# Token rows of x and B, and the samples' outputs, by VectorE 32x32 transposes instead of TensorE ones

## The chip, the cores and the metric

The kernel runs on one core of one Trainium2 chip (trn2). The metric is device time in microseconds of one execution, as the median of the runs. A core has five engines that run side by side, each with its own queue of instructions in order: TensorE (PE; its weight loads are listed as PEld), VectorE (DVE), ScalarE (ACT), GpSimd (POOL) and SyncE (SP), which here does nothing but issue DMAs. On-chip data lie in SBUF, 128 partitions wide; TensorE writes only to PSUM, which has eight banks.

## The reference, cut to what matters

One step of a hybrid layer on 336 tokens: 16 learned meta tokens, 256 prompt tokens and 8 samples of 8 tokens. After an RMS norm, one projection gives all inputs of two branches. Branch A is a Mamba-2 scan: 64 heads of 64 values in 8 groups; a group shares B and C (128 states). x, B and C first go through a causal convolution of width 4 and a SiLU.

```python
def ssd_chunked(xs, dt, log_a, bm, cm, h0, chunk):
    ...
    acum = jnp.cumsum(log_a.astype(f32).reshape(bsz, nc, chunk, ng, hr), axis=2)
    seg = acum[:, :, :, None] - acum[:, :, None, :]
    decay = jnp.exp(jnp.where(causal, seg, -jnp.inf))
    cb = jnp.einsum('bcign,bcjgn->bcijg', cc, bc)
    wts = cb[..., None] * decay * dtc[:, :, None]
    y_diag = jnp.einsum('bcijgr,bcjgrp->bcigrp', wts, xc)
    to_end = jnp.exp(acum[:, :, -1:] - acum) * dtc
    chunk_states = jnp.einsum('bcjgr,bcjgrp,bcjgn->bcgrpn', to_end, xc, bc)
    ...
    y_off = jnp.einsum('bcign,bcgrpn->bcigrp', cc, h_in) * jnp.exp(acum)[..., None]
    y = (y_diag + y_off).reshape(bsz, length, nh, hp).astype(xs.dtype)
```

The prompt is scanned as one segment of 16 and two of 128 tokens; each sample is a segment of 8 with its own initial state `h0`, which adds `y_off`. The states are carried from chunk to chunk (`h_in`). The output is normed, gated, projected, and merged with branch B (a short gated convolution); then come an output projection, a residual and a final norm. All tensors are float32.

## The kernel before

**Layout.** Activations are kept with features on the partitions and the 336 tokens along the free dimension. A projection unit (`unit`, `proj`) makes 128 output features: two weight blocks of 128x1024, each a DMA on SP (`wblk`, L92) into one of three buffers, split into a high part by ScalarE (L94) and a low part by VectorE (L96), and then 24 matmuls a block: 16 with the high part (L111, L112) and, after them, 8 with the low one (L115).

**The scan.** Phase B (pool `pb`) runs over 8 groups. The scan of group g, the generator `ssd(g, st)`, is a list of steps, woven by `weave` between the projection units: four gate units z of group g (8 weight blocks), the output projection of group g-1 (8 blocks), and the convolved inputs of group g+1 (B, C and four x tiles, `conv_tile`, 12 blocks). `NSTEP` = 23 steps are spread over the units by their weights; `behind` puts a step's instructions after the last weight split and the last matmul traced ahead of them, on the same engines. DMAs on SP are not held back by it: the planner of the language orders them by when their data and buffers are ready and by program order, so that a load of a later step can be issued early.

**Rows.** The sums over tokens need x and B with tokens on the partitions. The tokens are cut in three chunks `CH` of 128, 128 and 80. `rows(c)` (L526 to L549) transposes the four x tiles on TensorE against the identity into one PSUM bank (L531), B into another (L533), and beside it puts the products of B and C of the chunk (L534). VectorE multiplies x by dt into `xdt[c]` (L536); ScalarE and VectorE make a high and a low part of B, `bt[c]` (L543, L544), or a plain copy for chunk 2 (L539); the products are masked into `cbm[c]` (L548). `decay(c)` makes exp of the differences, `weights(c)` multiplies it with `cbm[c]` (L563) and makes `xe` from `xdt` on GpSimd (L565), `halve(c)` splits `xe`, `state(c)` makes the chunk's state (L582), `carry(c)` decays the one before.

**Samples.** C of each sample's 8 tokens lies in a zero-padded tile `CZ` (L512). Eight matmuls with 32 columns of `CZ` against the eight initial states (L632) give outputs with tokens on the partitions, four side by side in PSUM; they are scaled by `eaY` (L635), transposed by TensorE (L646), and added to `ys` (L652). `eaY` is made once in `tables` with a selection matrix at `C_SE` (L424).

## Time and profile before

| | |
|---|---|
| median of 3 runs | 1825.38 us (1825.02 to 1825.8) |
| span of the profiled execution | 1824.0 us; the page gives no other time of it |
| PE busy | 1817.0 us, 12640 matmul records |
| DVE, ACT, POOL busy | 1136.7, 828.8, 374.8 us |
| DMA | 331.35 MB, mean 182 GB/s; the SP queue's packets take 54.6% of 16 engines' span |
| one group of the scan | about 112 us (1039 to 1151 us, say) |

The page's first part gives busy time per engine, the fourth the chain of work that ended last. In a line of the timeline the first number is the start in the span, the second the time from first start to last end, then engine, line of the program, operation, out<-in, shapes, and in brackets how long the engine was idle before and what ended that. A matmul's own duration holds its way through the array, so that matmuls in a row start much closer than they last. "SPq" rows are DMA issues: the time is the issue's, not the transfer's. In the DMA view, the last number is the median from issue to landing.

### The profile page before, as it was taken

The numbers are of one execution on the slowest core, as the hardware profiler recorded it, in microseconds if no ns is written. First come the engines' busy times: TensorE is split into PE (matmuls) and PEld (weight loads), VectorE is DVE, ScalarE is ACT, GpSimd is POOL, SyncE is SP. The second block draws the span as 40 slices with busy tenths as digits, with TensorE's granted clock in tenths as the row PEclk, the third lists the DMA queues.
The fourth block names the chain that finished last, engine by engine and source line by source line (L and its number), as shares of the span: only waits on it lengthen the run. The fifth ranks groups of instructions, "written<-read, shape, count | busy, mean of one in ns | idle before, by whom it ended". The sixth has DMA issues, their size and how long they took to land.

```text
span 1824.0 us, 31666 instructions
## 1 busy us (share of the span) xinstructions
PE 1817.0 (100%) x12640; PEld 1791.5 (98%) x12640; DVE 1136.7 (62%) x1687; ACT 828.8 (45%) x1269; POOL 374.8 (21%) x406
## 2 busy tenths in 40 slices
PE   9999999999999999999999999999999999999998
PEld 9999999999999999999999999999999999999998
DVE  7745544444543335657587787876868778776544
ACT  6433333333333334645656354564536546343543
POOL 0000000000000001143152432424334242400012
PEclk9999999999999999999999999999999999999999
DMA  7444444444444446456566574665746657576553
GB/s 256 143 152 150 151 149 149 144 152 152 156 152 161 162 162 224 151 182 230 168 201 225 174 248 150 205 215 178 244 150 217 201 167 252 159 236 213 183 176 127
DMA packets 117283, 331.35 MB, mean 182 GB/s; under 512 B 20816, under 2 KB 37904, under 8 KB 117136
## 3 DMA queue, kind: packets, MB, share of 16 engines
q1 hardware_dynamic: 116272, 327.96, 54.6%
q8 instruction: 99, 1.62, 0.3%
q10 hardware_dynamic: 864, 1.38, 0.2%
q14 instruction: 48, 0.39, 0.1%
HBM read 296.41 MB, written 32.88 MB: 181 GB/s over the span
## 4 chain that ended last, share of the span: by engine, by line
PE 98%; ACT 1%; DMA 0%; issue 0%; DVE 0%; POOLq 0%; POOL 0%; ACTq 0%; DVEq 0%
PE pj L111 30%; PE pj L112 30%; PE pj L115 30%; PE yb L642 2%; PE pj L219 1%; PE ms L632 1%; PE yb L582 1%; PE pj L857 1%; PE ms L531 1%; DMA wraw<-w 0%; PE ms L219 0%; PE yb L708 0%; PE yb L883 0%; PE ms L646 0%; PE ms L188 0%; ACT W L556 0%
## 5 line engine op out<-in xcount | busy, mean ns | idle before, releaser
L111 PE MATMUL pj<-hx,whi 128*128 128x320 f32 (+3 forms) x2880 | 864.2, 312 | 0.0
L112 PE MATMUL pj<-hx,whi 128*128 128x320 f32 (+3 forms) x2880 | 860.6, 311 | 0.0
L96 DVE TENSOR_TENSOR wlo<-wraw,whi 128x1024 fp32r<-128x1024 f32 x470 | 591.3, 1259 | 417.3 <-PE pj L115 214.8
L94 ACT ACTIVATE whi<-wraw 128x1024 fp32r<-128x1024 f32 x470 | 497.0, 1058 | 773.7 <-PE pj L112 639.6
L111 PEld LDWEIGHTS pj<-hx,whi 128*128 128x128 f32 x2880 | 540.7, 188 | 3.8 <-ACT pad L457 1.7
L112 PEld LDWEIGHTS pj<-hx,whi 128*128 128x128 f32 x2880 | 541.5, 188 | 0.1
L115 PE MATMUL pj<-hx,wlo 128*128 128x320 f32 (+3 forms) x2880 | 485.4, 310 | 0.0
L115 PEld LDWEIGHTS pj<-hx,wlo 128*128 128x128 f32 x2880 | 440.5, 188 | 0.0
L111 PE MATMUL pj<-yh,whi 128*128 128x320 f32 x512 | 153.5, 312 | 0.1
L112 PE MATMUL pj<-yl,whi 128*128 128x320 f32 x512 | 152.2, 308 | 0.0
L593 POOL TENSOR_TENSOR h<-h,decS 128x512 f32<-128x512 f32 x64 | 72.5, 1166 | 152.2 <-PE ms L632 152.2
L111 PEld LDWEIGHTS pj<-yh,whi 128*128 128x128 f32 x512 | 96.6, 189 | 1.4 <-ACT zs L498 0.4
L112 PEld LDWEIGHTS pj<-yl,whi 128*128 128x128 f32 x512 | 95.9, 187 | 0.6
L115 PE MATMUL pj<-yh,wlo 128*128 128x320 f32 x512 | 95.7, 309 | 0.0
L739 DVE TENSOR_TENSOR yan<-yan,pj 128x320 f32<-128x320 f32 x112 | 54.3, 485 | 64.6 <-PE pj L115 63.1
L242 POOL COPY SCS<-up 128x2 f32<-128x2 f32 x16 | 18.2, 1139 | 359.2 <-DVE up L236 329.0
L466 DVE SCALAR_TENSOR_TENSOR cacc<-pad,V,cacc 128x360 f32<-128x360 f32 (+1 forms) x144 | 89.0, 618 | 2.0
L115 PEld LDWEIGHTS pj<-yh,wlo 128*128 128x128 f32 x512 | 80.3, 188 | 0.0
L459 POOL COPY pad<-cs 128x24 f32<-128x24 f32 x48 | 49.5, 1032 | 128.3 <-DVE cacc L466 116.9
L111 PE MATMUL pj<-vhi,whi 128*128 128x320 f32 x256 | 75.5, 308 | 0.0
L112 PE MATMUL pj<-vlo,whi 128*128 128x320 f32 x256 | 75.5, 308 | 0.0
L460 POOL COPY cs<-pad 128x3 f32<-128x3 f32 x48 | 45.3, 944 | 81.5 <-ACT pad L457 81.1
(287 smaller groups left out, 1710.9 us busy)
## 6 DMA issues: line engine op xcount, KB each, us to landing
wraw<-w SPq DMA_DIRECT2D x346, 512.0 KB, 3.8
wraw<-wso SPq DMA_DIRECT2D x64, 512.0 KB, 3.5
wraw<-wsc SPq DMA_DIRECT2D x32, 512.0 KB, 3.7
h<-h0T SPq DMA_DIRECT2D x32, 512.0 KB, 5.5
ssms<-h SPq DMA_DIRECT2D x32, 512.0 KB, 4.3
wraw<-wo SPq DMA_DIRECT2D x32, 512.0 KB, 3.8
xq_d<-xe SPq DMA_DIRECT2D x16, 320.0 KB, 3.4
W<-ac_d SPq DMA_DIRECT2D x8, 576.0 KB, 6.5
```

The costliest lines, as they stand in the source:

```text
L94: latest["act"] = nc.scalar.activation(hi[:, :n], raw[:, :n], AF.Copy).ins
L96: latest["dve"] = nc.vector.tensor_tensor(lo[:, :n], raw[:, :n], fb(hi[:, :n]), sub).ins
L111: nc.tensor.matmul(out, w, xh(k0 + k), start=first and k == 0, stop=False)
L112: nc.tensor.matmul(out, w, xl(k0 + k), start=False, stop=False)
L115: latest["pe"] = nc.tensor.matmul(out, w, xh(k0 + k), start=False, stop=last and k == nk - 1).ins
L219: nc.tensor.matmul(pu[i][:, :T - t0], w[:, o:o + P], x[:, k, t0:], start=k == 0 and j == 0, stop=k == 15 and j == 2)
L459: nc.gpsimd.tensor_copy(smp[:, :, 0:3], cs[:, 1:9, :])
L460: nc.gpsimd.tensor_copy(cs[:, 0, :], pad[:, 272:275])
L466: nc.vector.scalar_tensor_tensor(acc[:, i0:], pad[:, i0 + k:360 + k], col(V_CW, 4 * j + k), acc[:, i0:], mult, add)
L593: nc.gpsimd.tensor_tensor(split(h0[b]), split(h0[b]), bc(hv(decS[:, b, :], g), [P, 8, HP]), mult)
L642: nc.tensor.matmul(yb[q * HP:(q + 1) * HP, t, t0:t0 + n], x[:, h * HP:(h + 1) * HP], w[:, h, :], start=i == 0, stop=i == 3)
L739: nc.vector.tensor_tensor(ya[:, m, :TV], ya[:, m, :TV], pp[:, :TV], add)
```

## The change

It takes the transposes of x, B and the samples' outputs off TensorE.

1. In `conv_tile`, after B or an x tile (128 features x 336 tokens) is made, VectorE transposes it block by block, 32x32: tokens 0 to 319 in one instruction, the last 32 in a second, into the 352 columns of the tile `acc`. This tile is written to DRAM, `xr_d`, as 4 blocks of 32 rows of 1408 bytes, by a DMA on ScalarE's queue. The DMA is held in `pend` and issued by `flush` one unit later, behind an activation of the next `conv_tile` or z unit.
2. `load(c)` reads it back by 32 tokens: for each, 32 partitions x 16 pieces of 32 floats of x into `xdt[c]`, and 32 x 4 pieces of B into `bt[c]`; 22 DMAs a group on SP, traced in the fifth step, behind `decay(1)`, which moves there from the sixth.
3. `rows(c)` is parted. `cross()` makes all three products of B and C in one PSUM bank and masks them into three tiles `cbm`; `rows_in(c)` multiplies `xdt[c]` by dt in place and splits `bt[c]`. For chunk 0 it stands ahead of `weights(0)`, for chunk 1 behind `halve(0)`, for chunk 2 behind `halve(1)`.
4. The samples' outputs are made by 32 matmuls of 128 columns, so that each 32-partition block of PSUM holds one head quarter's 32 features with the tokens in its rows; scaled over 256 columns, transposed by VectorE and added from SBUF. `CZ` and `eaY` get the layout for it; `eaY` is made by eight small matmuls with columns of the identity, and the matrix at `C_SE` goes.

```diff
+    xr_d = [dr.tile([20, 32, XR], F32, name=f"xr_d{i}") for i in range(2)]
...
-            nc.tensor.matmul(pc[:, 0:NH], CM[:80, C_SE:C_SE + P], eat[:80, 2, :], start=True, stop=True)
-            nc.vector.tensor_copy(eaY, pc[:, 0:NH])
+            for c in range(2):
+                for a in range(0, P, 32):
+                    nc.tensor.matmul(pc[a:a + 32, NH * c:NH * c + NH], ident[:80, META + 32 * c:META + 32 * c + 32],
+                                     eat[:80, 2, :], start=True, stop=True)
...
+        def flush():
+            while pend:
+                nc.scalar.dma_start(*pend.pop())
...
             nc.scalar.activation(acc[:, i0:], pad[:, i0:360], AF.Identity, bias=col(V_CB, j), scale=col(V_CW, 4 * j))
+            flush()
...
+            if rows is not None:
+                nc.vector.transpose(acc[:, :320], out[:, :320])
+                nc.vector.transpose(acc[:, 320:XR], out[:, T - 32:])
+                pend.append((rows.rearrange("a q n -> (a q) n"), acc[:, :XR]))
...
                 nc.scalar.activation(z[:, :TV], pz, AF.Copy)
+                flush()
...
-            def rows(c):
-                (t0, n), m = CH[c], NT[c]
-                pp = ps.tile([P, 512], F32, name="ms")
-                for t in range(4):
-                    nc.tensor.transpose(pp[:n, t * P:t * P + P], xs[:, t, t0:t0 + n], ident)
-                pq = ps.tile([P, 512], F32, name="ms")
-                nc.tensor.transpose(pq[:n, 0:P], BT[:, t0:t0 + n], ident)
-                nc.tensor.matmul(pq[:n, P:P + m], BT[:, t0:t0 + n], CT[:, TGT[c]:TGT[c] + m], start=True, stop=True)
...
+            def load(c):
+                xdt[c] = big("xdt", 3)
+                b = bt[c] if c == 2 else fb(bt[c][:, 1, :])
+                rows = xr_d[g % 2].rearrange("a q n -> q a n")
+                for i in range(4 if c < 2 else 3):
+                    k, a, q = 4 * c + i, 32 * i, 16 if 4 * c + i == 10 else 0
+                    for d, lo, n in ((xdt[c], 0, 16), (b, 16, 4)):
+                        nc.sync.dma_start(d[a:a + 32 - q].rearrange("p (a f) -> p a f", f=32),
+                                          rows[q:, lo:lo + n, 32 * k:32 * k + 32])
+
+            def cross():
                 pq = ps.tile([P, 512], F32, name="ms")
+                o = 0
+                for c, (t0, n) in enumerate(CH):
+...
+                    nc.tensor.matmul(q, BT[:, t0:t0 + n], CT[:, TGT[c]:TGT[c] + m], start=True, stop=True)
+                    cbm[c] = pb.tile([P, m], F32, name=f"cbm{c}", bufs=1)
+...
+            def rows_in(c):
+                n = CH[c][1]
+                nc.vector.tensor_tensor(split(xdt[c][:n]), split(xdt[c][:n]), bc(hv(dtt[:n, c, :], g), [n, 8, HP]), mult)
+                if c < 2:
+                    b = fb(bt[c][:, 1, :])
+                    nc.scalar.activation(bt[c][:, 0, :], b, AF.Copy)
+                    nc.vector.tensor_tensor(bt[c][:, 1, :], b, fb(bt[c][:, 0, :]), sub)
...
             yield
-            rows(0)
+            cross()
             yield
             decay(0)
             yield
             nc.scalar.activation(E, W[1], AF.Exp)
-            rows(1)
...
             yield
+            decay(1)
+            for c in range(3):
+                load(c)
+            yield
+            rows_in(0)
             weights(0)
             yield
             halve(0)
-            decay(1)
-            yield
-            rows(2)
+            rows_in(1)
             yield
             carry(0)
             state(0, pieces(0))
             weights(1)
             yield
             halve(1)
+            rows_in(2)
             decay(2)
...
-            for s_ in range(2):
-                for q in range(4):
-                    nc.tensor.matmul(po[32 * q:32 * q + 32], CZ[:, 64 * q + 32 * s_:64 * q + 32 * s_ + 32],
-                                     h0[2 * q + s_], start=s_ == 0, stop=s_ == 1)
+            for b in range(NB):
+                z = 160 * (b // 4) + 32 * (b % 4)
+                for a in range(4):
+                    nc.tensor.matmul(po[32 * a:32 * a + 32, P * (b // 4):P * (b // 4) + P], CZ[:, z:z + 32],
+                                     h0[b].rearrange("p (t a f) -> p a t f", a=4, f=32)[:, a],
+                                     start=b % 4 == 0, stop=b % 4 == 3)
...
+            nc.vector.transpose(yo[:, 256:], yo[:, :256])
...
-            for t in range(4):
-                nc.tensor.transpose(pt_[:, t * P:t * P + P], yo[:, t * P:t * P + P], ident)
...
+            sy = ys[:, :, 272:].rearrange("p t (s q) -> p t s q", q=32)
+            nc.vector.tensor_tensor(sy, sy, yo[:, 256:].rearrange("p (s t q) -> p t s q", s=2, t=4), add)
```

More of the change, by code (lines that the diff above doesn't have):

```diff
@@ L164, in tile_hybrid_step @@
     eat = keep.tile([P, 3, NH], F32, name="eat")
-    eaY = keep.tile([P, NH], F32, name="eaY")
+    eaY = keep.tile([P, 2, NH // 2], F32, name="eaY")
     cdec = keep.tile([P, 2, NH], F32, name="cdec")
@@ L423, in tables @@
             pc = ps.tile([P, 512], F32, name="ms")
-            nc.tensor.matmul(pc[:, 0:NH], CM[:80, C_SE:C_SE + P], eat[:80, 2, :], start=True, stop=True)
-            nc.vector.tensor_copy(eaY, pc[:, 0:NH])
+            for c in range(2):
+                for a in range(0, P, 32):
+                    nc.tensor.matmul(pc[a:a + 32, NH * c:NH * c + NH], ident[:80, META + 32 * c:META + 32 * c + 32],
+                                     eat[:80, 2, :], start=True, stop=True)
+            for i in range(2):
+                nc.vector.tensor_copy(eaY[64 * i:64 * i + 64], pc[64 * i:64 * i + 64, :2 * NH].rearrange(
+                    "p (c h i) -> p i c h", c=2, i=2)[:, i])
             yield
@@ L447, in tile_hybrid_step, with conv_tile @@
         npad = [0]
-        CZ = pb.tile([P, 256], F32, name="CZ", bufs=1)
+        CZ = pb.tile([P, 320], F32, name="CZ", bufs=1)
         nc.gpsimd.memset(CZ, 0.0)
-        czs = CZ.rearrange("p (q w) -> p q w", w=64)
-        def conv_tile(src, j, t0, out, cs):
+        czs = CZ.rearrange("p (s i w) -> p s i w", s=2, w=40)
+        pend = []
+        def flush():
+            while pend:
+                nc.scalar.dma_start(*pend.pop())
+        def conv_tile(src, j, t0, out, cs, rows=None):
             pp = proj(src, t0)
@@ L517, in ssd @@
             ys = pb.tile([P, 4, T], F32, name="ys", bufs=1)
-            W, xdt, xe, bt, cbm, hst = ([None] * 3 for _ in range(6))
+            W, xdt, xe, cbm, hst = ([None] * 3 for _ in range(5))
             W[0], W[1] = (pb.tile([P, 8, PX], F32, name="W")[:, :, :n] for n in (P - META, PX))
@@ new lines, in ssd @@
+            bt = [pb.tile([P, 2, P], F32R, name="bh0", bufs=1), free[:, 1024:1280].rearrange("p (i n) -> p i n", n=P),
+                  pb.tile([P, P], F32, name="bt", bufs=1)]
+            def load(c):
[7 more added lines that the diff above has]
+                                          rows[q:, lo:lo + n, 32 * k:32 * k + 32])
@@ new lines, in cross @@
+            def cross():
+                pq = ps.tile([P, 512], F32, name="ms")
+                o = 0
+                for c, (t0, n) in enumerate(CH):
+                    m = NT[c]
+                    q = pq[:n, o:o + m]
+                    o += m
+                    nc.tensor.matmul(q, BT[:, t0:t0 + n], CT[:, TGT[c]:TGT[c] + m], start=True, stop=True)
+                    cbm[c] = pb.tile([P, m], F32, name=f"cbm{c}", bufs=1)
+                    u0 = META if c == 0 else 0
+                    for a, b, to in ((0, m, 0),) if c < 2 else ((META, 80, 0), (0, META, 64)):
+                        nc.vector.tensor_tensor(cbm[c][:n, to:to + b - a], q[:, a:b],
+                                                U[:, u0 + a:u0 + b] if c < 2 else UQ[:, a:b], mult)
```

44 lines of the change are left out of this document (12 added, 32 removed).

## The prediction

> **What bounds the kernel now.** I read the page first (busy shares, granted clock, chain), then the stretch 1039 to 1151 us, one of eight like groups.
>
> ```profile
> PE 1817.0 (100%) x12640; PEld 1791.5 (98%) x12640; DVE 1136.7 (62%) x1687; ACT 828.8 (45%) x1269; POOL 374.8 (21%) x406
> PEclk9999999999999999999999999999999999999999
> PE 98%; ACT 1%; DMA 0%; issue 0%; DVE 0%; POOLq 0%; POOL 0%; ACTq 0%; DVEq 0%
> 1039.00:1151.00 112.00, 112.00 (x797) 108.99 (x796) 85.83 (x134) 58.46 (x100) 41.37 (x42) 1.00 0.61 199
> ```
>
> TensorE (PE) is busy for 1817.0 of 1824.0 us at full clock, and the chain of waits lies on it for 98%. In a group's 112 us it has no gap, while DVE works 85.8 and the DMA engines 61%. A matmul taken away shortens the run by its pitch, unless a wait fills the place. So I need the pitch of what goes, and the margins of the engines that get work.
>
> **What goes from PE.** Next the groups of the lines in question, and PE's timeline (start, duration) around `rows(1)` and the samples' output of one group.
>
> ```profile
> L531 PE MATMUL ms<-CR,xs x96: 270/272/273, 751.9 to 1550.4; 128*128 128x128 f32 x64, 128*80 128x128 f32 x32
> L533 PE MATMUL ms<-CR,BT x24: 272/273/273, 752.4 to 1550.5; 128*128 128x128 f32 x16, 128*80 128x128 f32 x8
> L646 PE MATMUL ms<-CR,xe x32: 272/273/328, 803.1 to 1579.5; 128*128 128x128 f32 x32
> ...
> 1095.04 0.60 PE L531 MATMUL ms<-CR,xs 128*128 128x128 f32 x4
> 1095.47 0.27 PE L533 MATMUL ms<-CR,BT 128*128 128x128 f32 x1
> 1095.58 0.41 PE L534 MATMUL ms<-CT,BT 128*128 128x144 f32 x2
> ...
> 1133.25 1.92 PE L632 MATMUL ms<-h,CZ 128*32 128x512 f32 x16
> 1135.11 0.66 PE L642 MATMUL yb<-W,xdt 128*64 128x112 f32 x8
> 1138.56 0.66 PE L646 MATMUL ms<-CR,xe 128*128 128x128 f32 x4
> 1138.97 0.40 PE L111 MATMUL pj<-hx,whi 128*128 128x336 f32 x1
> ```
>
> The 272 ns are latency; the pitch counts. From 1095.04 to 1095.58 five transposes take 0.54 us: 108 ns each. L646's four take 0.41. The counts, 96 + 24 + 32, are 152 transposes, 19 a group: 19 x 0.108 = 2.05 us, times 8 = **16.4 us** removed. The products of B and C (L534) stay, gathered in `cross()`.
>
> **The samples' state product (L632)** becomes 32 matmuls of 128 columns instead of 8 of 512: the same columns in 64 records (each float32 matmul is two) instead of 16. Now the block takes 1135.11 - 1133.25 = 1.86 us for 4 rounds of 4 records side by side, 0.46 a round. Lower bound: 16 rounds at a quarter of that, 1.86, no change. Upper bound: L642's pace, whose 64 records take 1138.56 - 1135.11 = 3.45 us, 54 ns each: 64 x 54 ns = 3.45, 1.6 more a group, 12.7 us in all. I take 0: L642's 54 ns are mostly streaming, and the records of a round already run side by side.
>
> The Trainium skill ("TensorE: Matmul & The Clock Gate", "Wait — 56ns, not 53.3ns?") gives a floor of about 25 ns start to start, or 62 ns per MATMUL when its sequencer decodes in software. By 25 ns the estimate stays at no change; by 62 ns, 64 x 62 = 4.0 us, 2.1 more a group, and the whole gain is gone. The trace's 54 ns over 64 records speak against the 62.
>
> In `tables`, once, one 64-column matmul becomes eight, four side by side: I add 0.1 us.
>
> **What DVE gains.** For B and the four x tiles, a transpose of 128x320 and one of 128x32 follow each convolution. No such instruction is in the trace. DVE is tightest here:
>
> ```profile
> 1051.77 0.49 DVE L696 TENSOR_SCALAR ms_x<-ms 128x320 f32<-128x320 f32 x1 [1.11 <-ACT ms_r L695]
> ...
> 1056.96 0.44 DVE L470 SCALAR_TENSOR_TENSOR xs<-cth,cacc 128x272 f32<-128x272 f32 x1
> ...
> 1063.55 0.44 DVE L470 SCALAR_TENSOR_TENSOR xs<-cth,cacc 128x272 f32<-128x272 f32 x1
> 1063.90 0.22 DVE L471 SCALAR_TENSOR_TENSOR xs<-cth,cacc 128x64 f32<-128x64 f32 x1
> ...
> 1065.36 1.22 DVE L96 TENSOR_TENSOR wlo<-wraw,whi 128x1024 fp32r<-128x1024 f32 x1
> ...
> 1067.64 1.39 PE L115 MATMUL pj<-hx,wlo 128*128 128x336 f32 x8
> ```
>
> From 1051.77 on DVE's rows follow without a gap; the weight block's low half is ready at 1066.58 and PE takes it up at 1067.64: 1.06 us of margin. Two x tiles end in this run, so two pairs of transposes come ahead of L96. By the 128x320 row (0.49) and the 128x64 row (0.22, about 0.14 to the next start) a pair is some 0.5, two are 1.0: just covered. At half that, nothing; at twice, 2.0, PE stalls 0.9 a group for seven groups, 6.6 us. I take 0, as these are plain passes of the same width. The rest of DVE's change is small: `rows_in` multiplies in SBUF what L536 multiplied from PSUM, and the output's second transpose takes the place of nothing on PE's path, since `ys` is wanted much later.
>
> **ScalarE** loses a copy (L539, chunk 2's B) and gains five DMA issues a group. Each waits for the transposes of the tile before, queued one unit later, so ACT's splits behind it are hardly held; by SP's rows an issue is 0.3 to 0.5 us, 2.5 at most in 112 of which ACT works 58. That is cover enough.
>
> **The loads** are the real risk. Per group: 22 DMAs on SP, 336 tokens x 20 pieces = 6720 pieces of 128 bytes. They need the last x tile, whose write is issued behind ACT's z copy (L498). Around that point:
>
> ```profile
> 1082.21 0.43 ACT L498 ACTIVATE zs<-pj 128x320 f32<-128x320 f32 x1
> ...
> 1083.31 1.63 SPq L604 DMA_DIRECT2D h<-h0T  x2
> 1085.04 0.38 SPq L92 DMA_DIRECT2D wraw<-w  x1
> 1086.49 0.33 SPq L92 DMA_DIRECT2D wraw<-wso  x1
> 1086.87 1.01 SPq L478 DMA_DIRECT2D cs<-convst  x1
> 1090.11 9.81 SPq L92 DMA_DIRECT2D wraw<-wso  x3
> ...
> 1093.32 1.06 ACT L94 ACTIVATE whi<-wraw 128x1024 fp32r<-128x1024 f32 x1 [4.84 <-DMA wraw<-w]
> ...
> 1094.41 1.23 DVE L96 TENSOR_TENSOR wlo<-wraw,whi 128x1024 fp32r<-128x1024 f32 x1 [2.95 <-ACT whi L94]
> 1095.56 2.18 DVE L563 TENSOR_TENSOR W<-W,cbm 128x896 f32<-128x896 f32 x1
> 1098.33 1.23 DVE L96 TENSOR_TENSOR wlo<-wraw,whi 128x1024 fp32r<-128x1024 f32 x1 [0.60 <-ACT whi L94]
> ...
> 1104.05 0.75 PE L115 MATMUL pj<-yh,wlo 128*128 128x320 f32 x4
> 1108.31 0.75 PE L115 MATMUL pj<-yh,wlo 128*128 128x320 f32 x4
> ```
>
> ```profile
> DMA packets 771, 0.35 MB, mean 202 GB/s; under 512 B 768, under 2 KB 768, under 8 KB 771
> q1 hardware_dynamic: 771, 0.35, 71.4%
> xh<-xq_d SPq DMA_DIRECT2D x16, 256.0 KB, 4.1
> SPq L92 <- DMA wraw<-w: 20.6, 12, 2.8
> ```
>
> The DMA view is of 1488.25 to 1490, when almost only W's 448-byte rows move: 768 packets in 1.75 us are 439 per us. At this pace 6720 pieces take 15.3 us; scaled by bytes (128/448) 4.4. I expect 8, nearer the short end, as the engines were busy 71% of that time with packets 3.5 times as long. SP's own issuing takes 22 x 0.4 to 0.53 (two xh issues took 1.06 together), 9 to 12 us, so the weight issue of 1090.11 goes out at 1098 or so.
>
> When do they land? The write is issued at 1082.7 and is there by 1087. ACT's wait at 1093.32 shows the queue still delivering what was issued at 1085. So chunk 0's eight DMAs (2560 pieces) come in from about 1094, in 2 to 6 us: 1096 to 1100. `rows_in(0)` and `weights(0)` would stand on DVE where L563 stands, at 1095.56, and wait 0.5 to 4.5 us. Behind them is the low half now done at 1099.56, wanted by PE at 1104.05: 4.5 us of cover, less 0.7 for the multiply moved there. The weight block sent at 1098 instead of 1090 lands near 1102 to 1105; ACT's split (1.06) ends by 1106; PE starts it 1.2 before 1108.31, at 1107.1. Both margins hold by a little. I take 0.2 us of stall for each of seven groups, 1.4 (bounds 0 and 4 a group, in the rivals). If the loads are still later, the late thing is first DVE's low half, then the state product of chunk 0.
>
> Moving `decay(1)` ahead of `halve(0)` and the loads changes only ACT's order within one gap; `czs` needs one POOL copy less.
>
> **Sum.** The page gives no time of the profiled execution beside its span, 1824.0; the runs' median, 1825.38, is 1.4 above. Span: 1824.0 - 16.4 + 0.1 + 1.4 = 1809.1; with the 1.4 around it, **1810.5 us**.
>
> **Rivals.**
>
> *Loads a little later.* With the long price of a piece, DVE waits until 1100, and the weights and the low half each come about 1.2 us after PE wants them. 8 x 1.2 = 9.6 in place of 1.4: 1818.7. For it: ACT already waits up to 4.84 us for weights in this stretch. Against it: the planner moves DMAs forward wherever data and buffers allow (B's half is written five units earlier).
>
> *SP's queue is held (the other side).* The row "SPq L92 <- DMA wraw<-w" shows SP waiting up to 2.8 us for the landing of an earlier weight DMA although the buffer is freed by DVE: the number of transfers under way is limited, and no moment of this trace has more than eight. 22 small loads are then three rounds of a landing each, 4.1 by the xh row and more under load, say 5.2: 15.6 us from 1087, and the weights of 1090.11 go out at 1103, land at 1108.5 with the pieces still moving, are split at 1109.6 or later, and PE, due at 1107.1, stalls 2.5 to 5. From a stall of 2.05 us a group on the gain is gone; at 3.75 it is 8 x 3.75 - 16.3 = 13.7 slower, 1839. For it: 22 DMAs in one place, and DMA busy already. Against: about 5 us of cover on both engines.
>
> The Trainium skill ("DMA: Bandwidth & Descriptors", "Rules for kernel authors") speaks for this rival: coalesce small transfers, since below 64 KB one pays mostly overhead; each load here is 64 or 16 KB. The trace agrees that a small load lands no sooner than a weight block.
>
> *Small matmuls at 54 ns a record*: 1810.5 + 12.7 = 1823.2.
>
> *No effect.* The place of the transposes fills with waits, so the change doesn't do what it says: 1825. Against it: no gap on PE today, and all waits of its operands have margin.
>
> **How the numbers follow.** Forecast 0.50, own range 1808 to 1814 (the half and the double of DVE's price, 0 to 0.5 of stall); loads late 0.22; SP held 0.16; no effect 0.07; small matmuls 0.05. What a measurement here tells from no change is about 0.2%, 3.7 us. Faster than 1821.7: 0.50 + 0.22 = 0.72. Same: 0.07 + 0.05 = 0.12. Slower: 0.16. The range, 1807.5 to 1824, takes the forecast, the late loads and the small matmuls, and leaves out the held queue and half of the no-effect case; its low end is the full 16.4 with the first L646's longer step (0.06 a group, by its row of up to 328 ns) and no stall, 1808.6, less 1 us for what another set of runs may differ by.
>
> **What would show it.** Right: no 128x128 transposes on PE in the scan, PE busy some 16 us less with the idle time unchanged at 7 us, the state product still 1.9 us a group, a transpose pair near 0.5 us. Wrong: PE waiting in front of the units L111 or L115 for ACT or DVE once a group, behind a DVE or ACT wait for xdt's DMA; SP holding weight issues behind the loads for over 12 us; a state product of 3 us.

## The result, and the profile after

The changed kernel takes 1891.07 us (median of four runs, 1889.84 to 1895.21) against 1825.22 before in the same session. The ratio is 1.0363, with a 95% interval of 1.0350 to 1.0375: slower by 66 us, where 1810.5 was forecast. The changed program's lines are numbered anew: weight DMA L94, its ScalarE part `whi` L96, its VectorE part `wlo` L98, matmuls L113, L114 (high) and L117 (low), products of `cross()` L565, their masks L569, row loads L555, rows times dt L574, z units L516 (tanh), L517 and L519, and L773, the `yan` additions of VectorE that take a finished PSUM tile of the output projection and free it. In the kernels of the experiments these numbers shift by a few lines.

The page of the changed kernel, whose span is 1888.5 us: busy times, and the granted clock in 40 slices:

```profile
PE 1833.5 (97%) x12886; PEld 1809.0 (96%) x12886; DVE 1183.9 (63%) x1776; ACT 828.8 (44%) x1261; POOL 376.6 (20%) x398
PEclk9999999999999999999999989999999999999999
```

TensorE's idle time went from 7 us (1824.0 - 1817.0) to 55 (1888.5 - 1833.5). And its busy time *rose* by 16.5 us although 152 transposes had left it. The waits of TensorE say where the idle time is (who waits for whom, total us, times, longest):

```profile
PE ms L565 <- DVE cbm L569: 23.4, 14, 2.4
PE pj L113 <- ACT whi L96: 15.1, 9, 1.8
PE pj L113 <- DVE yan L773: 7.8, 5, 1.6
PE pj L113 <- ACT zs L517: 1.9, 1, 1.9
```

So there are two places, both new. **The products**: 23.4 us, twice a group in seven groups, ahead of the second and third product of `cross()`. **The weight pieces** (the first matmuls of a weight block): 15.1 + 7.8 + 1.9 = 24.8 us, once or twice a group, nearly all just behind the last z unit. Together 48.2 us.

The first place, on the timeline of the group at 1104 us:

```profile
1104.84 0.37 PE L565 MATMUL ms<-CT,BT 128*128 128x112 f32 x2
...
1106.45 1.22 DVE L98 TENSOR_TENSOR wlo<-wraw,whi 128x1024 fp32r<-128x1024 f32 x1 [0.56 <-ACT whi L96]
1107.55 2.63 POOL L596 TENSOR_TENSOR E<-E,CT 128x1152 f32<-128x1152 f32 x1 [7.58 <-ACT E L629]
1107.60 0.27 DVE L569 TENSOR_TENSOR cbm<-ms,CR 128x112 f32<-128x112 f32 x1
1107.92 0.51 PE L565 MATMUL ms<-CT,BT 128*128 128x144 f32 x2 [2.11 <-DVE cbm L569]
1108.15 2.38 DVE L519 SCALAR_TENSOR_TENSOR zs<-cth,zs 128x320 f32<-128x320 f32 x1 [0.29 <-ACT zs L517]
1110.45 0.30 DVE L569 TENSOR_TENSOR cbm<-ms,CR 128x144 f32<-128x144 f32 x1
1110.80 0.55 PE L565 MATMUL ms<-CT,BT 128*80 128x80 f32 x2 [1.74 <-DVE cbm L569]
1113.37 2.33 PE L117 MATMUL pj<-hx,wlo 128*128 128x320 f32 x8
```

The first product is done at 1105.2. Its mask stands in VectorE's queue behind a weight split and runs at 1107.60. Only then does the second product start, in the same PSUM tile but other columns; then the same once more, this time behind a z product of VectorE that takes 2.38 us while GpSimd works (0.48 is its usual time). The last row shows what follows: eight low-half matmuls take 2.33 us where eight take 1.39 in the prediction's row of before, with some more columns. The windows around it (length, PE busy, granted clock, DMA share, GB/s):

```profile
1108.00:1110.00 2.00, 1.07 (x6) 0.71 1.08 285
1110.00:1112.00 2.00, 1.20 (x5) 0.50 0.56 77
1112.00:1114.00 2.00, 2.00 (x9) 0.50 0.39 62
1114.00:1116.00 2.00, 2.00 (x10) 0.59 0.58 91
```

The granted clock falls to 0.50 for some 7 us and is back at 1.00 from 1116 on. The list of cores gives its mean over the span: 0.983, where it was 0.999 before. So 1888.5 x 0.017 = 32 us are lost to the clock against 2. The account of the 64.5 us between the two spans: - 16.2 for the transposes (2.03 a group, shown further on) + 48.2 idle + 30 clock = + 62; 2.5 stay unassigned.

The second place, as rows of SyncE's, ScalarE's and TensorE's timelines of that group:

```profile
1106.29 9.47 SPq L555 DMA_DIRECT2D xdt<-xr_d  x11
1115.86 1.52 SPq L94 DMA_DIRECT2D wraw<-wso  x3
...
1126.31 0.44 ACT L516 ACTIVATE cth<-pj 128x320 f32<-128x320 f32 x1 [6.25 <-PE pj L117]
1126.96 1.06 ACT L96 ACTIVATE whi<-wraw 128x1024 fp32r<-128x1024 f32 x1
...
1128.07 0.41 PE L113 MATMUL pj<-yh,whi 128*128 128x320 f32 x1 [1.80 <-ACT whi L96]
1134.99 0.39 PE L113 MATMUL pj<-yh,whi 128*128 128x320 f32 x1 [1.53 <-DVE yan L773]
```

Eleven loads of x rows take SyncE 9.5 us, and the first weights of the output projection (`wso`) are issued behind them, 12.2 us ahead of the first matmul that uses them, its gap included; in before it is 16.4 us, from the issue at 1086.49 to the first such matmul at 1102.87. Their split stands in ScalarE's order *behind* the tanh of the last z tile, which must wait for TensorE: ScalarE is idle for 6.25 us, and TensorE then for 1.80.

### The profile page after: what moved, and what is told of

It is laid out like the page before. It is cut to its first block, busy times and chain, and to the rows that moved or that the text cites. A ratio compares the mean times of both kernels' runs of the same rounds, so it can differ in the third digit from the quotient of the medians.

```text
span 1888.5 us, 32627 instructions
## 1 busy us (share of the span) xinstructions
PE 1833.5 (97%) x12886; PEld 1809.0 (96%) x12886; DVE 1183.9 (63%) x1776; ACT 828.8 (44%) x1261; POOL 376.6 (20%) x398
## 4 chain that ended last, share of the span: by engine, by line
PE 87%; DVE 5%; ACT 3%; DMA 3%; issue 2%; SPq 0%; POOLq 0%; DVEq 0%; POOL 0%; ACTq 0%
PE pj L113 27%; PE pj L117 27%; PE pj L114 27%; DMA wraw<-w 2%; PE yb L679 1%; ACT whi L96 1%; DVE h L745 1%; DVE zs L519 1%; DVE wlo L98 1%; PE ms L665 1%; PE pj L221 1%; DVE cacc L480 1%; PE yb L611 1%; DVE xdt L574 1%; PE pj L891 0%
## 5 line engine op out<-in xcount | busy, mean ns | idle before, releaser
L113 PE MATMUL pj<-hx,whi 128*128 128x320 f32 (+3 forms) x2880 | 870.9, 314 | 4.3 <-ACT whi L96 4.3
L114 PE MATMUL pj<-hx,whi 128*128 128x320 f32 (+3 forms) x2880 | 866.3, 313 | 0.0
L98 DVE TENSOR_TENSOR wlo<-wraw,whi 128x1024 fp32r<-128x1024 f32 x470 | 598.1, 1274 | 378.7 <-PE pj L117 201.7
L96 ACT ACTIVATE whi<-wraw 128x1024 fp32r<-128x1024 f32 x470 | 496.0, 1058 | 751.3 <-PE pj L114 609.7
L113 PEld LDWEIGHTS pj<-hx,whi 128*128 128x128 f32 x2880 | 545.4, 189 | 9.5 <-ACT whi L96 5.0
L114 PEld LDWEIGHTS pj<-hx,whi 128*128 128x128 f32 x2880 | 546.2, 190 | 0.1
L117 PE MATMUL pj<-hx,wlo 128*128 128x320 f32 (+3 forms) x2880 | 491.0, 313 | 0.0
L117 PEld LDWEIGHTS pj<-hx,wlo 128*128 128x128 f32 x2880 | 445.3, 190 | 0.7
L113 PE MATMUL pj<-yh,whi 128*128 128x320 f32 x512 | 158.5, 320 | 20.5 <-ACT whi L96 10.8
L114 PE MATMUL pj<-yl,whi 128*128 128x320 f32 x512 | 157.0, 317 | 0.0
L113 PEld LDWEIGHTS pj<-yh,whi 128*128 128x128 f32 x512 | 100.2, 196 | 24.8 <-ACT whi L96 12.4
L114 PEld LDWEIGHTS pj<-yl,whi 128*128 128x128 f32 x512 | 100.1, 196 | 0.7
L117 PE MATMUL pj<-yh,wlo 128*128 128x320 f32 x512 | 99.9, 318 | 0.0
L472 POOL COPY pad<-cs 128x24 f32<-128x24 f32 x48 | 61.4, 1280 | 141.4 <-DVE cacc L480 116.3
L773 DVE TENSOR_TENSOR yan<-yan,pj 128x320 f32<-128x320 f32 x112 | 54.2, 484 | 54.5 <-PE pj L117 53.0
L117 PEld LDWEIGHTS pj<-yh,wlo 128*128 128x128 f32 x512 | 83.9, 196 | 0.2
L113 PE MATMUL pj<-vhi,whi 128*128 128x320 f32 x256 | 75.5, 308 | 0.0
L114 PE MATMUL pj<-vlo,whi 128*128 128x320 f32 x256 | 75.5, 308 | 0.0
L519 DVE SCALAR_TENSOR_TENSOR zs<-cth,zs 128x320 f32<-128x320 f32 x32 | 27.9, 871 | 65.2 <-ACT zs L517 64.8
```

The source lines that it names most:

```text
L96: latest["act"] = nc.scalar.activation(hi[:, :n], raw[:, :n], AF.Copy).ins
L98: latest["dve"] = nc.vector.tensor_tensor(lo[:, :n], raw[:, :n], fb(hi[:, :n]), sub).ins
L113: nc.tensor.matmul(out, w, xh(k0 + k), start=first and k == 0, stop=False)
L114: nc.tensor.matmul(out, w, xl(k0 + k), start=False, stop=False)
L117: latest["pe"] = nc.tensor.matmul(out, w, xh(k0 + k), start=False, stop=last and k == nk - 1).ins
L472: nc.gpsimd.tensor_copy(smp[:, :, 0:3], cs[:, 1:9, :])
```

## The experiments

**1. The products first.** My theory: the two places are independent, and the clock follows the gaps. First, `cross()` with its three products ahead of the masks:

```diff
                 nc.tensor.matmul(q, BT[:, t0:t0 + n], CT[:, TGT[c]:TGT[c] + m], start=True, stop=True)
+                    qs.append((c, n, m, q))
+                for c, n, m, q in qs:
                     cbm[c] = pb.tile([P, m], F32, name=f"cbm{c}", bufs=1)
```

> The changed kernel with one edit: the three products of a group are issued one behind the other, and the masks follow; nothing else is touched. Theory: the changed kernel loses 23.4 us of TensorE idle because the second and third product wait for VectorE's mask of the one before, which shares its PSUM tile, and 24.8 us because the output projection's weight pieces are split late; TensorE's busy time rose by 16.5 us although 16.4 us of transposes left, so 32.9 us are a lower clock behind those 48.2 us of gaps, 0.68 us for each. The products' gaps go and their clock with them: 1891 - 23.4 x 1.68 = 1852 us. Rival A (the clock is held down by something other than the gaps): only the idle time comes back, 1868 us. Rival B (the weights are late in any case, so TensorE stands still a little later for as long): 1885 to 1891 us, and the idle at the weight pieces grows by some 20 us.

Measured: 1855.41 us, ratio 1.0173 (1.0156 to 1.0190). Rows of the groups:

```profile
L113 PE MATMUL pj<-hx,whi 128*128 128x320 f32 (+3 forms) x2880 | 864.7, 312 | 6.5 <-ACT whi L96 6.5
L113 PE MATMUL pj<-yh,whi 128*128 128x320 f32 x512 | 157.6, 319 | 24.3 <-DVE yan L775 13.3 <-ACT whi L96 10.8 <-ACT yan L773 0.2
L565 PE MATMUL ms<-CT,BT 128*128 128x112 f32 (+2 forms) x48 | 6.2, 265 | 0.0
```

The products wait for nothing now (23.4 to 0.0), the clock rises to 0.994, and 35.7 us come back. Rival B allowed 6 and rival A, the gaps alone, 23.4; the theory said 39. The weight pieces' 24.8 us became 30.8, so it seems that a part of the wait moved there.

**2. The gathered products alone**, in the kernel before:

```diff
             yield
+            cross()
             rows(0)
```

(`rows(c)` without its product and masks, all else as before.)

> The kernel before with one part of the change alone: the three products of a group gathered into one step and one PSUM tile with the masks between them, as the change has it; transposes, rows and samples' outputs as before. Theory: two gaps a group of 1.0 to 2.4 us appear ahead of the second and third product and the clock falls behind them: 1825 + 23.4 x 1.68 = 1865 us. Rival (the mask comes late only because VectorE's order is upset by the rows that are read back): VectorE does each mask as soon as its product is done, gaps of 0.6 to 0.9 us, 16 of them, 10 to 14 us with no more than as much clock: 1837 to 1848 us. Rival (the clock has another cause): 1825 + 23 = 1848 us with the clock at 1.00.

Measured: 1839.80, ratio 1.0077 (1.0062 to 1.0092). Its group row, and windows around two of its gaps (PE busy, clock, DMA share, GB/s):

```profile
L552 PE MATMUL ms<-CT,BT 128*128 128x112 f32 (+2 forms) x48 | 9.5, 279 | 11.6 <-DVE cbm L556 11.5
...
1096.00:1098.00 2.00, 2.00 (x12) 0.61 0.94 369
1098.00:1100.00 2.00, 2.00 (x9) 0.54 0.05 20
...
1550.00:1552.00 2.00, 0.42 (x3) 1.00 0.97 365
1552.00:1554.00 2.00, 2.00 (x17) 1.00 0.96 363
```

This one part costs 14.4 us in a kernel with nothing else changed: the size of the first rival, not my 40, though by other gaps than it said. There is one a group, seven of 1.25 to 2.10 us, and just one of them (2.10, at 1095) is followed by the low clock. The gap of 1.92 at 1551 isn't. So my price of 0.68 us of clock for each us of gap was wrong as a rule: in these traces the clock's loss comes in pieces, and not behind every gap (last section).

**3. The samples' outputs alone**, in the kernel before (part 4 of the change, with `eaY` and `CZ`).

> The kernel before with one part of the change alone: the samples' outputs by 32x32 transposes on VectorE, with the state product cut into 128-column pieces; x and B rows as before. Theory: 32 transposes of 108 ns leave TensorE, 3.5 us, the state product keeps its 1.9 us a group, one VectorE transpose of about 0.4 us is covered: 1825.2 - 3.5 = 1821.8 us. Rival (the small matmuls cost 54 ns each instead of 30): 1834 us. Rival (VectorE's transpose stands between the product and what follows): TensorE waits once a group, 1826 to 1832 us.

Measured: 1823.99, ratio 0.9990 (0.9981 to 1.0000): 1.4 us gained of 3.5 forecast. The interval just reaches no change, but all ten runs (1823.0 to 1824.7) lie below the thirteen of before (1824.99 to 1827.07). TensorE's idle time is 0.3 us more. A group without a wait is 0.36 us shorter (111.44 us between state products, 111.80 before), 2.9 us in eight; against that the first state product starts 0.4 us later, and two of the groups are 0.3 and 0.7 us longer than the others. The state product is 15.6 us in all against 15.4 before, so the small matmuls cost nothing, as forecast.

**4. The loads on ScalarE's queue**, in the changed kernel:

```diff
-                        nc.sync.dma_start(d[a:a + 32 - q].rearrange("p (a f) -> p a f", f=32),
+                        nc.scalar.dma_start(d[a:a + 32 - q].rearrange("p (a f) -> p a f", f=32),
```

> The changed kernel with one edit: the 22 loads of rows a group are issued by ScalarE's queue instead of SyncE's. Theory (the weight pieces are late because SyncE's queue is held for 9.5 us by eleven loads ahead of them, and the pieces are then split behind the last z tile): SyncE's weight issues come some 9 us earlier, most of the 24.8 us of idle at the weight pieces goes with 0.68 us of clock for each: about 1850 us, the products' gaps of 23.4 us unchanged. Rival (the transfers themselves are late by contention of small packets, whoever issues them): 1885 to 1895 us. Rival (ScalarE is now held by its 22 issues of 0.45 us, and splits weights late): 1895 us or more, TensorE waiting for ScalarE.

Measured: 1951.39, ratio 1.0691 (1.0674 to 1.0708), clock 0.969. The second rival. ScalarE's timeline:

```profile
1156.22 0.31 ACT L577 ACTIVATE bh<-bh 128x128 fp32r<-128x128 f32 x1 [7.25 <-DMA xdt<-xr_d]
```

For 7.25 us it issues loads, and the split of TensorE's next weights, at 1156.43, stands behind them: a gap of 8.8 to 9.7 us in each group.

**5. Queue or order?** From here on the kernels have the products first (1855.41 us is what to compare with), but for two in the last experiment. Three loads' steps instead of one; then, the other way, the first `wso` block fetched and split ahead of the last z tile's last matmuls:

```diff
             decay(1)
-            for c in range(3):
-                load(c)
+            load(0)
             yield
             rows_in(0)
             weights(0)
+            load(1)
...
+            load(2)
             carry(0)
```

```diff
             hi, lo = wblk(src[:, half * 1024:half * 1024 + 1024])
+            if half and hook:
+                hook()
...
+            def ahead():
+                S[g - 1]["w"] = wblk(wso[g - 1, 0])
```

> The kernel with the three products first (1855 us, 30.8 us of TensorE idle, all of it at the weight pieces), and one edit more: the rows of the three token groups are loaded in three steps of the scan instead of one, so that SyncE's queue never holds more than four x loads in a row. Theory (eleven x loads in a row, 9 us, hold the weight issues behind them): the first weights of the output projection are issued 5 to 6 us earlier, the idle at the weight pieces falls from 30.8 to 5 to 15 us, about 1832 us. Rival (the split is late because ScalarE's order has it behind the last z tile's activations, whenever the weights land): 30 us of idle stay, 1850 to 1857 us. Rival (the scan's later steps now wait for rows that land late): TensorE waits at the state products, over 1857 us.

> The kernel with the three products first, and one edit more: the first weights of the output projection are fetched and split ahead of the last z tile's last matmuls in the program's order, so that their ScalarE copy can stand ahead of that tile's activations. Theory of the order (ScalarE's order alone makes the gap of 1.80 us, once a group): these eight gaps, 14.4 us, go, and some of what follows: 1835 to 1842 us. Theory of the queue (the weights themselves are issued late, behind eleven x loads): they land no earlier, ScalarE now waits for them with the z tile's activations behind it, the gaps stay at 1 us or more: 1848 to 1858 us.

> Products first, loads in three steps, and the first weights of the output projection ahead of the last z tile's activations. With the loads spread alone, these weights had landed some 3 us before ScalarE took them up and the gaps of 1.80 us stayed (1859.6 us); with the order alone they were late (1842.8 us, idle 22 us). If queue and order each hold back one part: idle under 10 us, 1820 to 1828 us. If the order alone counts: as with the order alone, 1840 to 1845 us.

Measured: spread 1859.62 (1.0190, 1.0174 to 1.0205); ahead 1842.78 (1.0098, 1.0083 to 1.0113); both 1839.20 (1.0074, 1.0061 to 1.0088), with 21 us of idle at the weight pieces and the clock at 0.999. The spread kernel, SyncE's, ScalarE's and TensorE's rows:

```profile
1102.11 1.29 SPq L94 DMA_DIRECT2D wraw<-wso  x2
...
1109.17 0.44 ACT L516 ACTIVATE cth<-pj 128x320 f32<-128x320 f32 x1 [2.46 <-PE pj L117]
1109.82 1.06 ACT L96 ACTIVATE whi<-wraw 128x1024 fp32r<-128x1024 f32 x1
...
1110.93 0.41 PE L113 MATMUL pj<-yh,whi 128*128 128x320 f32 x1 [1.80 <-ACT whi L96]
```

Here the first weights were issued at 1102.1; the DMA view of that moment (1102.0 to 1102.5) has 3.9 us to their landing, so they lay there at 1106.0. Yet their split came at 1109.82, behind a z tile that ScalarE had waited 2.46 us for. The gap is the same 1.80. So in this kernel the *order* of ScalarE's queue makes that gap. The other edit wins 12.6 us, just above the range of its theory, but it turns more than that order: the first weights now go out at 1095.24, ahead of the eleven loads (from 1095.61 on), so that queue and order aren't parted by it. And neither edit nor both bring the idle time under 20 us; for both I had expected 1820 to 1828.

**6. Other ways to carry the rows.** The scatter into rows of tokens done by the write (ScalarE's queue, four transfers a tile), so that SyncE reads whole rows with eight loads; and GpSimd's queue for the 22 loads; each also with the order turned.

```diff
+                for a in range(4):
+                    pend.append((rows[:, 32 * a:32 * a + 32].rearrange("(k q) f -> q k f", q=32),
+                                 acc[32 * a:32 * a + 32, :XR].rearrange("q (k f) -> q k f", f=32)))
...
-                        nc.sync.dma_start(d[a:a + 32 - q].rearrange("p (a f) -> p a f", f=32),
+                        nc.gpsimd.dma_start(d[a:a + 32 - q].rearrange("p (a f) -> p a f", f=32),
```

> The kernel with the three products first, and one edit more: the scatter of 128 B pieces is moved from the read to the write. ScalarE's queue writes each tile in four transfers, straight to rows of tokens, spread over the convolution's tiles, and SyncE reads whole rows of 2048 and 512 B in eight loads a group instead of 22, four of them of x instead of eleven. Theory (SyncE's queue is held by the eleven x loads): held 2 us instead of 9, idle at the weight pieces from 30.8 to under 8 us with the clock back at 0.999: 1812 to 1822 us, below the kernel before. Rival (ScalarE's 20 issues of 0.32 us instead of five stand in the splits' way): 4.8 us of issues more a group on an engine that is 45% busy, TensorE waits 1 to 2 us a tile: 1840 to 1870 us. Rival (order on ScalarE, as above): 1850 us.

> The scatter moved to the write and the first weights of the output projection fetched and split ahead of the last z tile's last matmuls, both. If queue and order each hold back one part, this one has neither: no idle at the weight pieces, 1810 to 1814 us, TensorE's busy time about 1805 us. If one of the two alone made the gaps, it equals the run with that one edit within 3 us.

> Products first, and the 22 row loads of a group issued by GpSimd's queue instead of SyncE's. Theory (eleven x loads in a row hold SyncE's weight issues): the first weights of the output projection are issued right behind those of the last z tile, 9 us earlier, idle at the weight pieces from 30.8 to under 8 us: 1812 to 1825 us. Rival (the order on ScalarE makes the gaps whenever the weights land): the gaps of 1.80 us stay, eight of them, 14 us with some clock: 1838 to 1850 us. Rival (GpSimd's issues are dear, or its own products stand behind loads that wait for the rows to be written): xe and the products with E come late, TensorE waits at the state products or at the outputs: over 1850 us.

> Products first, row loads on GpSimd's queue, and the first weights of the output projection ahead of the last z tile's activations. By the theory of queue and order: no idle over 3 us in all, TensorE's busy time 1803 to 1807 us: 1810 to 1814 us, below the kernel before. By the theory of the queue alone: equal to the run with GpSimd's queue alone within 3 us. By GpSimd held: over 1850 us.

Measured: scatter 1886.31 (1.0331) and 1877.67 with the order; GpSimd 1871.31 (1.0246) and 1874.40 with the order. My theory missed all four; the two on GpSimd's queue lie in the rival that had over 1850 us, the scatter in none. SyncE's waits in the scatter kernel, and GpSimd's issues in the other (busy us, mean ns, idle before):

```profile
SPq L556 <- DMA xr_d<-cacc: 91.0, 18, 9.3
```

```profile
L555 POOL DMA_DIRECT2D xdt<-xr_d x88 | 56.0, 642 | 85.1 <-DMA h<-h0T 50.4 <-DMA xdt<-xr_d 18.2 <-DMA xr_d<-cacc 14.1
```

With fewer loads SyncE stands at them for 91 us in all, up to 9.3 at a time, until the rows are written; the weights stand behind. GpSimd stands still for 85 us ahead of the x loads, with its own work in order behind them. TensorE's waits in that kernel are put down to ScalarE's z copies (20.6 us) and VectorE's `yan` (16.1), not to GpSimd; how they come from its queue was not followed.

**7. Late rows?** Rows written a group earlier (nothing to wait for, and so x and B of another group in the states); the first use of the rows three steps later; the last x tile left to TensorE.

```diff
-                rows = xr_d[g % 2].rearrange("a q n -> q a n")
+                rows = xr_d[(g + 1) % 2].rearrange("a q n -> q a n")
```

> The kernel with the products first, and the 22 loads of a group read the rows that the group before left in DRAM (group 0 writes both buffers), so that x and B enter the scan's states with the rows of another group: the amount of work, the queues and the sizes stay, only the wait for rows just written goes. Theory (the rows land too late: written 1090.5, in DRAM 1095, loaded 1096 to 1105, multiplied from 1108): the loads are issued some 10 us earlier, ScalarE and VectorE no longer stand at the rows, idle from 30.8 to under 5 us: 1811 to 1818 us. Rival (22 loads of 128 B pieces hold SyncE's queue wherever they stand): the idle moves and stays above 15 us, 1835 to 1855 us.

> The kernel with the products first, and three empty steps between the loads and the first use of the rows; the scan has 26 steps instead of 23, and the first product with the rows stands behind the second block of the output projection instead of behind the last z tile. Theory (rows too late): 14 us more for them to land, so the splits of the first weights have no row step ahead of them: idle from 30.8 to 5 to 12 us, 1815 to 1832 us. Rival (SyncE's queue and ScalarE's order behind the last z tile): the gaps of 1.80 us stay, 1840 to 1855 us.

> The kernel with the products first, and the last of the four x tiles turned by TensorE as before, three transposes of 108 ns a group (2.6 us in all); the other three tiles and B by VectorE and the loads, each x load three quarters of its size. Theory (rows too late, and it is the tile written last that sets it): the rows are complete in DRAM 10 us earlier, the loads go out before the weights of the last z tile, idle from 30.8 to under 10 us: 1814 to 1828 us. Rival (number of loads): 1845 to 1858 us.

Measured: 1848.74 (1.0121), 1908.90 (1.0454) and 1850.20 (1.0135). The theory that the rows land too late falls: without that wait there are still 28.7 us of idle, where there were 30.8. They move, though: in the first of these kernels 18.5 us lie at the weights of the convolution and z units, where loads now stand between SyncE's weight issues. Three later steps made it worse, beyond both theory and rival: 63.8 us of idle, 23.3 of them for the low halves of VectorE. With one x tile left to TensorE 25.2 us stay, the time in the range of the rival.

```profile
L113 PE MATMUL pj<-hx,whi 128*128 128x320 f32 (+3 forms) x2880 | 868.0, 313 | 18.5 <-ACT whi L96 18.5
```

**8. x left out; the loads without the use; the use without the loads.** First the kernel before with part 4 and with B's rows as changed, but x's rows by TensorE (B loaded in the scan's first step). On it, x written and loaded as well, into a buffer that nobody reads. And from the other side, the kernel with the products first, with x neither transposed, written nor loaded:

```diff
-                nc.tensor.transpose(pq[:n, 0:P], BT[:, t0:t0 + n], ident)
+            for c in range(3):
+                load(c)
```

```diff
+            for c in range(3):
+                load_x(c)
             weights(0)
```

```diff
-                    for d, lo, n in ((xdt[c], 0, 16), (b, 16, 4)):
+                    for d, lo, n in ((b, 16, 4),):
...
-                nc.vector.tensor_tensor(split(xdt[c][:n]), split(xdt[c][:n]), bc(hv(dtt[:n, c, :], g), [n, 8, HP]), mult)
+                nc.vector.tensor_tensor(xdt[c][:n].rearrange("p (t u e) -> p t u e", u=2, e=HP),
+                                        xs[:n, :, t0:t0 + P].rearrange("p t (u e) -> p t u e", u=2),
```

> The kernel before with the samples' outputs and the rows of B as the change has them, B's rows loaded at the scan's first step; x stays with TensorE's transposes, and each product stays in its own chunk's step. Theory (it is the x rows, written just before the scan, and the gathered products that cost; B's rows are written a whole convolution earlier and nothing waits for them): 56 of the 152 transposes leave TensorE, 6 us less, no idle: 1825.3 - 6 = 1819 us, with the samples' part having given 1.4 of its 3.5 us perhaps 1821 us. Rival (any row load on SyncE's queue delays weights): idle at the weight pieces of 1 to 2 us a group, 1826 to 1840 us.

> The kernel with B's rows and the samples' outputs as the change has them (1821.7 us, no idle), and the x rows written and loaded too, at the step where the scan first uses x, into a buffer that nobody reads (the third token group's loads are cut to 320 columns); the scan goes on with TensorE's transposes of x. Theory Q (the eleven x loads hold SyncE's queue ahead of the weights, and weights issued late find no slack): 20 to 30 us of idle at the weight pieces, 1842 to 1855 us. Theory U (what costs is the use of the rows: ScalarE and VectorE stand at steps that need them, with weight splits behind): 1821 to 1826 us, no idle.

> The kernel with the products first, without the x rows' VectorE transposes, writes and loads: the scan multiplies the x tiles as they lie in SBUF, untransposed, in the rows' place (so the scan's results are not the reference's); B's rows, the steps and everything else as changed. Theory Q: no idle, TensorE busy about 1803 us, 1808 to 1814 us. Theory U: ScalarE and VectorE still run the new step order, idle of 15 to 30 us stays, 1828 to 1850 us.

Measured: **1821.67 us without x** (eleven runs, ratio 0.9979, 0.9970 to 0.9988): faster than both kernels, with 0.5 us of idle at the weight pieces. With x loaded and unused 1844.09 (1.0100, 1.0083 to 1.0117). With x used and not loaded 1836.09 (1.0059, 1.0036 to 1.0082). TensorE's waits in the second, and in the third at the output projection:

```profile
L113 PE MATMUL pj<-hx,whi 128*128 128x320 f32 (+3 forms) x2880 | 865.5, 312 | 4.4 <-ACT whi L96 4.4
L113 PE MATMUL pj<-yh,whi 128*128 128x320 f32 x512 | 156.1, 316 | 11.0 <-ACT whi L96 10.8 <-DVE yan L776 0.2
```

```profile
L113 PE MATMUL pj<-yh,whi 128*128 128x320 f32 x512 | 156.5, 317 | 14.1 <-DVE yan L779 13.0 <-ACT zs L517 1.2
```

Neither theory has it alone; each has one half. Writing and loading x, used by nobody, makes 15.4 us of idle, all but 0.2 for ScalarE's splits. The use, with no x loaded, makes 14.1, nearly all for VectorE's `yan`. Together 29.5, against 30.8 in the kernel that has both, and there the two waits are of these sizes by name as well: 17.3 for the splits and 13.3 for `yan`. This fits that no single edit above removed it. The two halves come from kernels with different steps, so that the sum comes out may be in part chance.

How loads that nobody reads make ScalarE late is in the queues of one group, first in the kernel that loads x, then in the one without x:

```profile
1093.36 7.93 SPq L560 DMA_DIRECT2D ys<-xr_d  x11
1106.81 0.44 ACT L515 ACTIVATE cth<-pj 128x320 f32<-128x320 f32 x1 [1.98 <-PE pj L117]
1107.46 2.95 ACT L96 ACTIVATE whi<-wraw 128x1024 fp32r<-128x1024 f32 x3
```

```profile
1100.05 1.06 ACT L96 ACTIVATE whi<-wraw 128x1024 fp32r<-128x1024 f32 x1 [1.26 <-PE pj L114]
1101.27 0.41 ACT L515 ACTIVATE cth<-pj 128x320 f32<-128x320 f32 x1
```

With the loads, the first weights of the output projection go out at 1101.38, behind all eleven, and three splits stand behind the last z tile's tanh. Without them these weights go out at 1085.37, and the splits (1095.10, 1097.74, 1100.05) stand ahead of that tanh. So the loads change both the issue and the order, and the spread kernel above shows that the order is enough for the gap. Why the planner turns it is in no trace.

What the use costs VectorE is in its groups (busy us, mean ns), the first line before, the others in the kernel that uses x and loads none; under them two rows of that kernel's timeline:

```profile
L536 DVE TENSOR_TENSOR xdt<-ms,dtt 128x512 f32<-128x512 f32 x16 | 10.9, 680 | 0.0
L577 DVE TENSOR_TENSOR xdt<-xs,dtt 128x512 f32<-128x512 f32 x16 | 18.7, 1170 | 0.0
L584 DVE TENSOR_TENSOR bh<-bh 128x128 fp32r<-128x128 f32 x8 | 8.2, 1029 | 0.0
...
1097.89 1.82 POOL L606 TENSOR_TENSOR xw<-xe,xw 128x512 fp32r<-128x512 f32 x1 [2.12 <-ACT xw L605]
1098.47 1.80 DVE L577 TENSOR_TENSOR xdt<-xs,dtt 128x512 f32<-128x512 f32 x1
```

The multiply by dt costs 7.8 us more, and the split of chunk 0's B, 2.2 us in before (274 ns each), 6.0. Reading x from SBUF instead of PSUM is not dearer by itself: alone, the multiply takes 0.69 us, as before. In seven of the eight groups chunk 1's starts while GpSimd works, and then it takes 1.80; so does the split of B (1.13 us beside GpSimd, 0.29 in the one group where GpSimd is nearly done). The `yan` additions, which read one operand from PSUM, take 0.48 us alone and beside GpSimd alike (88 and 24 of them). That fits that the operand's move out of PSUM lets GpSimd hold VectorE up, but in before no multiply by dt ran beside GpSimd, so for the multiply itself no run shows it. In the rows of this group VectorE works without a gap from 1097.33 until it comes to `yan` at 1105.80, and TensorE goes on at 1106.33. That these 13.8 us *are* the 14.1 of idle is not shown. The run with the use alone moved the order of the steps as well, and more work on VectorE does not make TensorE wait by itself: in the kernel without x the split of chunk 1's B takes 2.69 us a group instead of 0.28, 19 us more in all, with 0.5 us of idle. Where the work stands ahead of `yan` counts as well. The z product of VectorE, which took 2.38 us in the changed kernel's row at 1108.15, has little part in it: its mean is 481 ns in before, 871 in the changed kernel, and 519 here.

## Why the prediction was wrong

**The transposes: right.** A group without gaps takes 109.78 us in the kernel that uses x without loading it (none of the 19 transposes is left), and 111.81 before: 2.03 less, for 19 transposes at 108 ns forecast as 2.05. The starts of two successive state products, in that kernel and in the kernel before:

```profile
796.47 0.32 PE L671 MATMUL ms<-h,CZ 128*32 128x128 f32 x4
...
906.25 0.41 PE L671 MATMUL ms<-h,CZ 128*32 128x128 f32 x6
```

```profile
797.83 0.64 PE L632 MATMUL ms<-h,CZ 128*32 128x512 f32 x4
...
909.64 0.64 PE L632 MATMUL ms<-h,CZ 128*32 128x512 f32 x4
```

**The state product, the VectorE transposes, ScalarE's five issues: right.** The state product takes 15.6 us in all against 15.4; a pair of transposes takes 0.50 + 0.17 us, a third over the 0.5 forecast, and an issue 0.33; none of TensorE's waits names them.

**The step that failed first: the products "stay, gathered", at no cost.** I counted the matmuls and not the order in which they stand with their masks. Gathering three products into one PSUM tile, each followed by its mask, makes the next matmul wait for VectorE. I named no wait, no rival and no price there; it is 23.4 us of idle, and without it the changed kernel is 36 us faster, the clock included; alone, in the kernel before, it costs 14.4. The Trainium skill had a warning that I hadn't drawn on ("PSUM — Partial Sum Buffer", "PSUM bank collisions raise a hardware error"): TensorE's write and another engine's read of one bank must be kept apart by bank (strictly, by bank and block of 32 partitions), not by address. The trace fits it: the products write other columns than the masks read, and wait all the same, 14 times. That the program waits is shown; what the chip would do without the wait, no run here shows.

**The loads: the right mechanism in a rival at 0.16, with a wrong trace of it.** "SP's queue is held" is what one half of the remaining idle is: 15.4 us from writing and loading x alone, 1821.7 to 1844.1, 22 us slower where I gave the whole rival 13.7. The forecast went by landing times, with "both margins hold by a little", and took before's order of ScalarE's queue as given. What failed was that premise: that order is written by a planner, and in the changed kernel and the one that loads x unused the first weight splits stand behind the z tile's tanh, in before and in the one without x ahead of it. My 0.2 us a group is a gap of 1.80 for ScalarE's split in each of the eight groups, 24.8 us in all with VectorE's `yan`, and in the spread kernel the 1.80 stays even with the weights there. The sentence that a small load lands no sooner than a weight block was also read too fast: in before's DMA view loads of 32 and 64 KB land in 3.0 and 2.9 us, weight blocks of 512 KB in 3.4 to 3.8.

**"`rows_in` multiplies in SBUF what L536 multiplied from PSUM": costed at nothing too.** The mean of 680 ns became 1218 in the changed kernel, 0.68 alone and 1.5 to 1.8 us in the eight multiplies that ran beside GpSimd.

**The clock was not in the sum at all.** I had the granted clock as a constant, since no gap in the trace of before was long enough to show it move. It cost 30 us, nearly half of the result.

The list of what would show me wrong held in part: TensorE waits at the unit's matmuls for ScalarE or VectorE once a group. But SyncE's weight issues were held for 9.5 us, not over 12, ScalarE's wait ahead of the late split is for the z tile and not for the DMA of `xdt`, and the largest single wait was not on the list.

## What to carry to other kernels

Where an edit gathers work that was spread, write down the order on every engine that it makes, matmul by matmul and mask by mask: in this kernel a PSUM tile read between two writes to it was a wait, even at other columns. A transfer has to be priced where its queue stands, and each queue here carried something that TensorE needed: SyncE the weights, ScalarE the splits, GpSimd the scan's own products. Take of a change the parts that ask for no late data: here the rows of B and the samples' outputs are worth 3.5 us, while the rows of x cost more than they free in each of the ways tried.

## What the hardware did that I had not expected

A gap of TensorE of 2 us can cost about twice its length. After some of the gaps the granted clock falls to 0.50 for about 3.4 us (1.7 us lost), or for twice that; after others, nothing: 2.10 us at 1095 is followed by 0.61 and 0.54, 1.92 us at 1551 by 1.00, both in the kernel with the gathered products alone; and a gap of 3.05 us in the kernel with the products first, 3.9 us behind one of 1.80, is followed by full clock:

```profile
1346.00:1349.00 3.00, 0.08 (x1) 1.00 0.29 55
1349.00:1352.00 3.00, 3.00 (x21) 1.00 0.57 191
```

In the changed kernel each of the seven pairs of gaps at the products is followed by the low clock; of its eight gaps of 1.80 us, two are not. The Trainium skill ("TensorE: Matmul & The Clock Gate", "HAM oscillation — how this bites in real kernels") warns of gaps over some 3.4 us. The rows agree on half speed and on a period near 3.4 us, but not on the length: gaps under 2.2 us were enough here, and one of 3.05 was not.
